# Splitting dense products into 256-column halves, full-row score products, and merged value products in a two-layer encoder kernel

## The chip, the cores and the metric

The kernel runs on one core of a Trainium2 chip. The metric is the device time of one execution in microseconds (us); lower is better. The core's engines are named as in the profile: PE does matrix products, PEld is its load of the stationary operand (which overlaps PE), DVE and ACT do element-wise work, POOL is a third element-wise engine, SP only issues DMA transfers.

## What is computed

Two layers over 512 tokens of width 1024. Each layer is an attention block and a SwiGLU feed-forward block, each with an RMS norm ahead and a residual add behind; a last norm ends it.

```python
def reference(x, norm_mix, norm_ffn, w_qkv_a, w_out_a, sink_a, w_qkv_b, w_out_b,
              w_gate, w_up, w_down, norm_final):
    for i in range(DEPTH):                      # DEPTH = 2
        h = rmsnorm(x, norm_mix[i])
        j = i // 2
        if i % 2 == 0:
            x = x + window_gqa_sink(h, w_qkv_a[j], w_out_a[j], sink_a[j])
        else:
            x = x + dilated_mixture_attention(h, w_qkv_b[j], w_out_b[j])
        h = rmsnorm(x, norm_ffn[i])
        x = x + swiglu(h, w_gate[i], w_up[i], w_down[i])
    return rmsnorm(x, norm_final)

def swiglu(h, w_gate, w_up, w_down):            # 1024 -> 2816 -> 1024
    return (jax.nn.silu(h @ w_gate) * (h @ w_up)) @ w_down
```

Layer 0's attention has 16 query heads on 4 key heads of width 64, a window of 128 keys either side, a bias linear in distance and a sink logit per head. Layer 1's has 16 heads in three groups (near keys, every 4th, every 16th), merged by their softmax denominators.

## The kernel before

All data lies transposed, features in the 128 partitions and the 512 tokens along the row. Every float32 operand of a dense product is held as two float32r tiles, a high part and the rest: `xh, xl` for the normalised input, `oh, ol` for attention outputs, `ah, al` for the feed-forward's middle, `wh, wl` for weights. Weights arrive in 128x1024 pieces by a DMA from SP into `wraw`; `split` makes `wh` on ACT (L85) and `wl` on DVE (L86), three pieces deep.

`mm3` (L106) is every dense product: high by high, high by low, low by high, three matmuls into one PSUM bank. In `unit` (projections, gate, up) and in the down and output products the weights are stationary and 512 tokens stream, so L107 to L109 are 128x512 matmuls. In `values` (L178) the tokens are stationary and 256 weight columns stream, so they are 128x256 there; `final` (L438) also runs the last down product in two column halves.

The order on PE is written out by hand; the other engines' order comes from a scheduler. Attention is a list of small steps (scores, `turn` = transposes of probabilities, `weigh` = values times probabilities), and `weave` deals them out with a fixed number of dense pieces, the fill, spread evenly between the steps: with fewer steps each gap holds more fill. The feed-forward blocks are dense products without anything between.

`score_pair` (L126) computes two heads' scores. The 64 rows of a head hold the query's high part, the other 64 its low part (`split_queries`), so that one product over 128 rows with the key's high part in both halves gives two terms. The third, query high by key low, is a product over 64 rows (L130), whose low part `kl` is one tile for both heads. `weigh`, `weigh_a` and `weigh_b` multiply 64 value columns each, in plain float32, into the upper or lower half of the one PSUM bank `ov` (L366, L658, L662, L733). In layer 0 they come one key block at a time, in layer 1 one query tile or class at a time.

In the pool `const` the tiles lie in the order in which they are declared (L72 to L81). The weights' tiles lie behind them.

Of the kernel before, what the change touches and what calls it, by code (L numbers as in the profile page):

```python
# [14 lines left out]
S = 512  # L15
# [42 lines left out]
def trunk(ctx, tc, xT, gains, sink, tabs, qsc, wunits, wv, outT):  # L58
# [11 lines left out]
        return psum.tile([128, 512], F32, tag=tag, name=name or tag, bufs=BUFS[tag])  # L70

    x = const.tile([128, NK, S], F32, name="x")  # L72
    xh = const.tile([128, NK, S], F32R, name="xh")
    xl = const.tile([128, NK, S], F32R, name="xl")
    g_sb = const.tile([128, 5, NK], F32, name="g_sb")
    qs_sb = const.tile([128, 16], F32, name="qs_sb")
    sink_sb = const.tile([128, H], F32, name="sink_sb")
    nsink = const.tile([128, H], F32, name="nsink")
    tab = const.tile([128, 1024], F32, name="tab")
# [24 lines left out]
        return chunks(tiles, shape)  # L104

    def mm3(out, ah, al, bh, bl, first, last):  # L106
        nc.tensor.matmul(out, ah, bh, start=first, stop=False)  # L107
        nc.tensor.matmul(out, ah, bl, start=False, stop=False)  # L108
        nc.tensor.matmul(out, al, bh, start=False, stop=last)  # L109

# [9 lines left out]
    def split_keys(k, pair, low):  # L120
        for a, (own, other) in enumerate((HALVES, HALVES[::-1])):
            nc.scalar.activation(pair[a][own], k[own], AF.Copy)
            nc.scalar.activation(pair[a][other], pair[a][own].bitcast(F32), AF.Copy)
            nc.vector.tensor_tensor(low[own], k[own], pair[a][own].bitcast(F32), op=OP.subtract)

    def score_pair(outs, qp, kp, low, qc, kc, first=True):  # L126
        for a in range(2):
            nc.tensor.matmul(outs[a], qp[a][:, qc], kp[a][:, kc], start=first, stop=False, skip_group_check=True)  # L128
        for a, own in enumerate(HALVES):
            nc.tensor.matmul(outs[a], qp[a][own, qc], low[own, kc], start=False, stop=True, skip_group_check=True)  # L130

# [154 lines left out]
    with tc.tile_pool(name="l0", bufs=2) as pool:  # L286
# [5 lines left out]
        def k_unit(P, **kw):  # L292
            def done(ps):
                t = spool.tile([128, S], F32, name="tmp")
                nc.vector.tensor_tensor(t, ps, norm["rb"], op=OP.mult)
                qk["k", P] = [pool.tile([128, S], F32R, name=f"kt{a}") for a in range(2)]
                qk["kl", P] = pool.tile([128, S], F32R, name="kl")
                split_keys(t, qk["k", P], qk["kl", P])
            return unit(5 * P, xh, xl, "mm", done, **kw)

# [9 lines left out]
        def attention0(P, h, b):  # L310

            k0, k1 = max(128 * b - 128, 0), min(128 * b + 256, S)
            w = k1 - k0
            off = k0 - (128 * b - 128)
            nb = w // 128
            block = slice(128 * b, 128 * b + 128)
            own = slice(4 * P + 2 * h, 4 * P + 2 * h + 2)
            heads = [8 * P + 4 * hf + 2 * h + i for i in range(2) for hf in range(2)]
            st = {}

            def scores(i):
                if i == 0:
                    st["pr"] = pool.tile([128, 4, 385], F32, name="pr", bufs=3)
                    st["m"] = pool.tile([128, 3, 4], F32, name="mst", bufs=4)
                    for k in range(2):
                        at = heads[2 * k]
                        nc.gpsimd.tensor_copy(st["pr"][:, 2 * k:2 * k + 2, w], sink_sb[:, at:at + 5:4])
                pr, m = st["pr"], st["m"]
                es = slice(2 * i, 2 * i + 2)
                ps = [bank("sc")[:, :w] for _ in range(2)]  # L330
                score_pair(ps, qk["q", P, 2 * h + i], qk["k", P], qk["kl", P], block, slice(k0, k1))
                for hf in range(2):
                    e = 2 * i + hf
# [25 lines left out]

            def weigh(kb):  # L360
                if kb == 0:
                    st["ov"] = bank("ov")
                ov = st["ov"]
                for hf in range(2):
                    vs = slice(64 * (2 * P + hf), 64 * (2 * P + hf) + 64)
                    nc.tensor.matmul(ov[64 * hf:64 * hf + 64, :256], v0[:, k0 // 128 + kb, vs],  # L366
                                     st["pt", kb][:, 256 * hf:256 * hf + 256], start=(kb == 0), stop=(kb == nb - 1))
                if kb == nb - 1:
                    src = ov[:, :256].rearrange("p (i q) -> p i q", i=2)
                    nc.scalar.activation(oh[:, own, block], src, AF.Copy)  # L370
                    nc.vector.tensor_tensor(ol[:, own, block], src, oh[:, own, block].bitcast(F32),
                                            op=OP.subtract)

            rest = [lambda kb=kb: turn(kb) for kb in range(nb)]
            rest += [lambda kb=kb: weigh(kb) for kb in range(nb - 1)]
            return [lambda: scores(0), lambda: scores(1)], rest, lambda: weigh(nb - 1)


        gens = [k_unit(0, cuts=(0, 2, 4, 8))[1], q_unit(0, 0, cuts=(0, 4, 8))[1]]
# [170 lines left out]
    with tc.tile_pool(name="l1", bufs=2) as pool:  # L550
# [9 lines left out]
        def qk_units(p, g):  # L560
# [15 lines left out]
            def k_done(ps):  # L576
                name = "k1" if g else "ka"
                qk["k", p, g] = k = pool.tile([128, S], F32, name=name, bufs=2 if g else 1)
                out, src, rb = views(k, ps, norm["rb"])
                nc.vector.tensor_tensor(out, src, rb, op=OP.mult)  # L580
                if g == 0:
                    qk["ks", p] = [pool.tile([128, S], F32R, name=f"ks{a}", bufs=1) for a in range(2)]
                    qk["kl", p] = pool.tile([128, S], F32R, name="kl1", bufs=1)
                    split_keys(k, qk["ks", p], qk["kl", p])

            at = u1 + 6 * p + 2 * g
# [182 lines left out]
        def attention_a(p):  # L769

            pts = {}

            def turn(ts, t):
                pts[t] = turn_a(p, ts, t)

            return [lambda: scores_a(p, (0, 1)), 0, lambda: scores_a(p, (2, 3)), 0,
                    lambda: turn((0, 1), 0), lambda: turn((0, 1), 1), lambda: weigh_a(p, 0, pts[0]),
                    lambda: weigh_a(p, 1, pts[1]), lambda: turn((2, 3), 2), lambda: turn((2, 3), 3),
                    lambda: merge_turn(p), lambda: weigh_a(p, 2, pts[2]), lambda: weigh_a(p, 3, pts[3]),
                    lambda: merge_back(p)]  # L780

        def attention_b(p, pauses=(0, 0, 0, 0, 0)):
            pts = {}

            def turn(cs, c):
                pts[c] = turn_b(p, cs, c)

            return [lambda: scores_b(p, (0, 1)), pauses[0], 0, lambda: scores_b(p, (2, 3)), pauses[1],
                    lambda: turn((0, 1), 0), lambda: turn((0, 1), 1), pauses[2], lambda: weigh_b(p, 0, pts[0]),
                    lambda: weigh_b(p, 1, pts[1]), pauses[3], lambda: turn((2, 3), 2), lambda: turn((2, 3), 3),  # L790
                    pauses[4], lambda: merge_rows(p), lambda: weigh_b(p, 2, pts[2]),
                    lambda: weigh_b(p, 3, pts[3])]

        def out_part(j, lo, hi, ps={}, w={}):
            def gen():
# [134 lines left out]
```

## Time and profile before

| what | value |
|---|---|
| time, median of 3 runs | 1534.75 us (1534.73 to 1535.71) |
| time of the profiled execution | 1534.25 us |
| its span, first to last instruction | 1532.5 us |
| PE busy | 1516.9 us, 8038 matmuls |
| DVE busy | 721.7 us |
| ACT busy | 606.8 us |
| granted PE clock, mean over the span | 0.997 |
| DMA | 127.68 MB, mean 83 GB/s |

Durations of PE's matmuls overlap, since they are pipelined. What a matmul costs in a stream of its kind is the distance from its start to the next one's start; the timeline's first column has the starts. "x8" at a row's end merges that many matmuls of one line. A plain float32 matmul stands in the trace as two, so a step of four of them in the program is x8 there; transposes stand as one.

### The profile page before, as it was taken

To read this page: it belongs to the slowest core of one execution; us is meant where nothing else is said; L and a number is where in the kernel's file an instruction comes from. 1 tells how busy PE (TensorE), PEld (TensorE's weight loads), DVE (VectorE), ACT (ScalarE), POOL (GpSimd) and SP (SyncE) were. 2 spreads that over 40 slices of the span, in tenths; PEclk is the share of its full clock that TensorE was granted. 3 is DMA by queue.
4 is the path that set the end of the run, shared out by engine and by line. 5 is a ranking of instruction groups with operands and counts; after the bars stand their busy time and mean duration, and the time that the engine had idled before them with its cause. 6 is when DMAs were issued, how large, how long until landed. Compare 5 with 4: busy or idle time off the path is not lost.

```text
span 1532.5 us, 19975 instructions
## 1 busy us (share of the span) xinstructions
PE 1516.9 (99%) x8038; PEld 1212.6 (79%) x8038; DVE 721.7 (47%) x1360; ACT 606.8 (40%) x1106; POOL 107.9 (7%) x151
## 2 busy tenths in 40 slices
PE   9999999999999999999999999999999999999997
PEld 7666788888888889897887877778778888888886
DVE  6666544444443343335545545545464444443223
ACT  6656443222223244443544535535443222222221
POOL 3324200000000010000000000000020000000111
PEclk9999999999999999999999999999999999999999
DMA  5110222223222232222212122222132222222231
GB/s 193 56 51 19 83 84 96 97 96 96 96 86 90 96 100 83 89 65 82 70 56 83 56 83 70 69 70 70 55 97 83 96 96 96 96 91 92 90 100 55
DMA packets 38413, 127.68 MB, mean 83 GB/s; under 512 B 4528, under 2 KB 6832, under 8 KB 38320
## 3 DMA queue, kind: packets, MB, share of 16 engines
q1 hardware_dynamic: 36832, 125.08, 24.9%
q8 instruction: 63, 1.03, 0.3%
q10 hardware_dynamic: 1488, 1.33, 0.3%
q14 instruction: 30, 0.25, 0.1%
HBM read 124.29 MB, written 2.10 MB: 82 GB/s over the span
## 4 chain that ended last, share of the span: by engine, by line
PE 97%; DVE 1%; ACT 1%; issue 0%; DMA 0%; SPq 0%; DVEq 0%; ACTq 0%
PE mm L107 18%; PE mm L109 17%; PE mm L108 17%; PE sc L109 5%; PE sc L108 5%; PE sc L107 5%; PE psv L107 4%; PE psv L109 3%; PE psv L108 3%; PE tp L107 3%; PE tp L108 3%; PE tp L109 3%; PE ov L366 1%; PE sc L128 1%; PE sc L130 1%; PE ov L733 1%
## 5 line engine op out<-in xcount | busy, mean ns | idle before, releaser
L85 ACT ACTIVATE wh<-wraw 128x1024 fp32r<-128x1024 f32 (+3 forms) x239 | 246.4, 1034 | 588.2 <-PE mm L108 228.1
L86 DVE TENSOR_TENSOR wl<-wraw,wh 128x1024 fp32r<-128x1024 f32 (+3 forms) x239 | 288.9, 1210 | 202.8 <-ACT wh L85 202.8
L107 PE MATMUL mm<-xh,wh 128*128 128x512 f32 x816 | 341.2, 418 | 0.0
L109 PE MATMUL mm<-xh,wl 128*128 128x512 f32 x816 | 323.6, 397 | 1.5 <-DVE wl L86 1.5
L108 PE MATMUL mm<-xl,wh 128*128 128x512 f32 x816 | 323.0, 396 | 0.8 <-DVE xl L206 0.8
L107 PEld LDWEIGHTS mm<-xh,wh 128*128 128x128 f32 x816 | 154.0, 189 | 49.9 <-issue 16.7
L109 PEld LDWEIGHTS mm<-xh,wl 128*128 128x128 f32 x816 | 153.8, 188 | 38.5 <-DVE wl L86 2.2
L108 PEld LDWEIGHTS mm<-xl,wh 128*128 128x128 f32 x816 | 154.4, 189 | 30.9 <-DVE xl L206 3.0
L220 POOL TENSOR_TENSOR ssum<-ssum,tmp 128x512 f32<-128x512 f32 x34 | 55.4, 1628 | 1038.9 <-ACT tmp L216 1023.9
L107 PE MATMUL psv<-wh,xh 128*128 128x256 f32 x288 | 85.3, 296 | 0.0
L109 PE MATMUL psv<-wh,xl 128*128 128x256 f32 x288 | 81.0, 281 | 0.0
L108 PE MATMUL psv<-wl,xh 128*128 128x256 f32 x288 | 80.9, 281 | 0.0
L107 PE MATMUL mm<-ah,wh 128*128 128x512 f32 (+1 forms) x198 | 75.8, 383 | 0.0
L108 PE MATMUL mm<-al,wh 128*128 128x512 f32 (+1 forms) x198 | 75.6, 382 | 0.0
L109 PE MATMUL mm<-ah,wl 128*128 128x512 f32 (+1 forms) x198 | 75.6, 382 | 0.0
L107 PE MATMUL sc<-xh,wh 128*128 128x512 f32 x176 | 69.6, 396 | 0.0
L107 PE MATMUL tp<-xh,wh 128*128 128x512 f32 x176 | 69.6, 396 | 0.0
L108 PE MATMUL tp<-xl,wh 128*128 128x512 f32 x176 | 69.5, 395 | 0.0
L109 PE MATMUL sc<-xh,wl 128*128 128x512 f32 x176 | 69.5, 395 | 0.0
L109 PE MATMUL tp<-xh,wl 128*128 128x512 f32 x176 | 69.5, 395 | 0.0
L108 PE MATMUL sc<-xl,wh 128*128 128x512 f32 x176 | 69.5, 395 | 0.0
L107 PE MATMUL sc<-ah,wh 128*128 128x512 f32 (+1 forms) x176 | 66.9, 380 | 0.0
(174 smaller groups left out, 2431.2 us busy)
## 6 DMA issues: line engine op xcount, KB each, us to landing
wraw<-wunits SPq DMA_DIRECT2D x192, 512.0 KB, 3.3
wraw<-wv SPq DMA_DIRECT2D x26, 512.0 KB, 3.3
wraw<-wunits SPq DMA_DIRECT2D x16, 384.0 KB, 2.9
x<-xT SPq DMA_DIRECT2D x8, 256.0 KB, 5.0
wraw<-wunits SPq DMA_DIRECT2D x3, 256.0 KB, 5.5
outT<-x ACTq DMA_DIRECT2D x2, 384.0 KB, 2.7
tab<-tabs SPq DMA_DIRECT2D x1, 512.0 KB, 5.9
outT<-x ACTq DMA_DIRECT2D x2, 256.0 KB, 2.3
```

The source lines that it names most:

```text
L85: nc.scalar.activation(out_h, src, AF.Copy)
L86: nc.vector.tensor_tensor(out_l, src, out_h.bitcast(F32), op=OP.subtract)
L107: nc.tensor.matmul(out, ah, bh, start=first, stop=False)
L108: nc.tensor.matmul(out, ah, bl, start=False, stop=False)
L109: nc.tensor.matmul(out, al, bh, start=False, stop=last)
L128: nc.tensor.matmul(outs[a], qp[a][:, qc], kp[a][:, kc], start=first, stop=False, skip_group_check=True)
L130: nc.tensor.matmul(outs[a], qp[a][own, qc], low[own, kc], start=False, stop=True, skip_group_check=True)
L220: nc.gpsimd.tensor_tensor(norm["sum"], norm["sum"], sq, op=OP.add)
L366: nc.tensor.matmul(ov[64 * hf:64 * hf + 64, :256], v0[:, k0 // 128 + kb, vs], st["pt", kb][:, 256 * hf:256 * hf + 256], start=(kb == 0), s ...
L733: nc.tensor.matmul(ov[rows, 128 * c:128 * c + 128], vals[p // 2, 1 + g][:, c, hv + 64 * a:hv + 64 * a + 64], pt[:, 256 * a + 128 * g:256 * ...
```

## The change

There are four edits. `mm3` issues each 512-column matmul as two of 256 columns, with the same stationary operand for both. The 64-byte tile `qs_sb` is declared ahead of `xh`, so that `xh` and `xl` lie 64 bytes further on, while all tiles from `sink_sb` on, weights and pools included, lie where they lay. `kl` becomes two tiles with the key's low part in both halves of the rows (ACT copies it across), and `score_pair` runs four products over 128 rows, which also adds the term low by low. All of a unit's or a pair's `weigh` products are issued together, and steps are reordered for it.

```diff
     x = const.tile([128, NK, S], F32, name="x")
+    qs_sb = const.tile([128, 16], F32, name="qs_sb")
     xh = const.tile([128, NK, S], F32R, name="xh")
...
     def mm3(out, ah, al, bh, bl, first, last):
-        nc.tensor.matmul(out, ah, bh, start=first, stop=False)
-        nc.tensor.matmul(out, ah, bl, start=False, stop=False)
-        nc.tensor.matmul(out, al, bh, start=False, stop=last)
+        for k, (a, b) in enumerate(((ah, bh), (ah, bl), (al, bh))):
+            for c in range(0, out.shape[-1], 256):
+                cols = slice(c, c + 256)
+                nc.tensor.matmul(out[:, cols], a, b[:, cols], start=first and k == 0 and c == 0,
+                                 stop=last and k == 2, skip_group_check=True)
...
-            nc.vector.tensor_tensor(low[own], k[own], pair[a][own].bitcast(F32), op=OP.subtract)
+            nc.vector.tensor_tensor(low[a][own], k[own], pair[a][own].bitcast(F32), op=OP.subtract)
+            nc.scalar.activation(low[a][other], low[a][own].bitcast(F32), AF.Copy)
...
         for a in range(2):
-            nc.tensor.matmul(outs[a], qp[a][:, qc], kp[a][:, kc], start=first, stop=False, skip_group_check=True)
-        for a, own in enumerate(HALVES):
-            nc.tensor.matmul(outs[a], qp[a][own, qc], low[own, kc], start=False, stop=True, skip_group_check=True)
+            for k in (kp, low):
+                nc.tensor.matmul(outs[a], qp[a][:, qc], k[a][:, kc], start=first and k is kp, stop=k is low,
+                                 skip_group_check=True)
...
             return [lambda: scores_b(p, (0, 1)), pauses[0], 0, lambda: scores_b(p, (2, 3)), pauses[1],
-                    lambda: turn((0, 1), 0), lambda: turn((0, 1), 1), pauses[2], lambda: weigh_b(p, 0, pts[0]),
-                    lambda: weigh_b(p, 1, pts[1]), pauses[3], lambda: turn((2, 3), 2), lambda: turn((2, 3), 3),
-                    pauses[4], lambda: merge_rows(p), lambda: weigh_b(p, 2, pts[2]),
-                    lambda: weigh_b(p, 3, pts[3])]
+                    lambda: turn((0, 1), 0), lambda: turn((0, 1), 1), pauses[2], lambda: turn((2, 3), 2),
+                    lambda: weigh((0, 1)), pauses[3], lambda: turn((2, 3), 3), pauses[4],
+                    lambda: merge_rows(p), lambda: weigh((2, 3))]
```

`attention_a` is reordered in the same way (its two bursts stand behind the third transposes and at the end), and layer 0's `weigh` runs over all key blocks of a unit, behind the first transposes of the next unit.

The first scores of layer 0 on PE, before (kt are the keys' high parts, kl their low part, qt the queries; two heads are one pair of tiles):

```order
L128 MATMUL sc<-kt_278,qt_289 128x256
L128 MATMUL sc<-kt_279,qt_290 128x256
L130 MATMUL sc<-kl,qt_289 128x256
L130 MATMUL sc<-kl,qt_290 128x256
L107 MATMUL mm<-xh,wh 128x512
```

The same place now, with the dense row behind it:

```order
L133 MATMUL sc<-kt_350,qt_364 128x256
L133 MATMUL sc<-kl_352,qt_364 128x256
L133 MATMUL sc<-kt_351,qt_365 128x256
L133 MATMUL sc<-kl_353,qt_365 128x256
```

The two products over 64 rows at the end of each pair are gone; each head's two products now follow each other and share the stationary queries.

The last attention pass of layer 1 on PE (p = 7), from its transposes of probabilities (L720) on, before. L733 are the value products, L765 the transposes that merge the groups:

```order
L720 MATMUL tp<-ident,pr_9067 128x128 x8
...
L733 MATMUL ov<-pt_9165,v_8095 64x128 x2
L733 MATMUL ov<-pt_9165,v_8484 64x128 x2
L733 MATMUL ov<-pt_9172,v_8095 64x128 x2
L733 MATMUL ov<-pt_9172,v_8484 64x128 x2
...
L720 MATMUL tp<-ident,pr_9105 128x128 x8
```

And now, where L722 are the transposes and L735 the value products:

```order
L722 MATMUL tp<-ident,pr_12277 128x128 x8
...
L722 MATMUL tp<-ident,pr_12321 128x128 x4
L735 MATMUL ov<-pt_12399,v_11050 64x128 x2
L735 MATMUL ov<-pt_12399,v_11532 64x128 x2
L735 MATMUL ov<-pt_12406,v_11050 64x128 x2
L735 MATMUL ov<-pt_12406,v_11532 64x128 x2
...
L722 MATMUL tp<-ident,pr_12321 128x128 x4
```

The third transposes, which need the second pair of classes (pr_12321), moved ahead of the first value products. Between them and the first transposes stands one piece of fill; before, it was one piece, the value products and three more pieces.

The split of layer 0's first key and queries on ACT, before (L122 and L123 make the keys' high parts, L117 the queries'):

```order
L122 ACTIVATE kt_278<-tmp 64x512
L122 ACTIVATE kt_279<-tmp 64x512
L123 ACTIVATE kt_278<-kt_278 64x512
L123 ACTIVATE kt_279<-kt_279 64x512
L117 ACTIVATE qt_289<-tmp 64x512
```

And now:

```order
L125 ACTIVATE kt_350<-tmp 64x512
L125 ACTIVATE kt_351<-tmp 64x512
L126 ACTIVATE kt_350<-kt_350 64x512
L128 ACTIVATE kl_352<-kl_352 64x512
L126 ACTIVATE kt_351<-kt_351 64x512
L128 ACTIVATE kl_353<-kl_353 64x512
L120 ACTIVATE qt_364<-tmp 64x512
```

Two copies of low parts come in ahead of the queries, each of which waits for DVE's subtraction.

More of the change, by code (lines that the diff above doesn't have):

```diff
@@ L75, in trunk @@
     g_sb = const.tile([128, 5, NK], F32, name="g_sb")
-    qs_sb = const.tile([128, 16], F32, name="qs_sb")
     sink_sb = const.tile([128, H], F32, name="sink_sb")
@@ L296, in done @@
                 qk["k", P] = [pool.tile([128, S], F32R, name=f"kt{a}") for a in range(2)]
-                qk["kl", P] = pool.tile([128, S], F32R, name="kl")
+                qk["kl", P] = [pool.tile([128, S], F32R, name=f"kl{a}") for a in range(2)]
                 split_keys(t, qk["k", P], qk["kl", P])
@@ L358, in turn, with weigh @@
                     nc.scalar.activation(pt, tp, AF.Copy)
[L360 to L372, printed above, removed]
+            def weigh():
+                ov = bank("ov")
+                for kb in range(nb):
+                    for hf in range(2):
+                        vs = slice(64 * (2 * P + hf), 64 * (2 * P + hf) + 64)
+                        nc.tensor.matmul(ov[64 * hf:64 * hf + 64, :256], v0[:, k0 // 128 + kb, vs],
+                                         st["pt", kb][:, 256 * hf:256 * hf + 256], start=(kb == 0),
+                                         stop=(kb == nb - 1))
+                src = ov[:, :256].rearrange("p (i q) -> p i q", i=2)
+                nc.scalar.activation(oh[:, own, block], src, AF.Copy)
+                nc.vector.tensor_tensor(ol[:, own, block], src, oh[:, own, block].bitcast(F32), op=OP.subtract)
             rest = [lambda kb=kb: turn(kb) for kb in range(nb)]
-            rest += [lambda kb=kb: weigh(kb) for kb in range(nb - 1)]
-            return [lambda: scores(0), lambda: scores(1)], rest, lambda: weigh(nb - 1)
+            return [lambda: scores(0), lambda: scores(1)], rest, weigh
         gens = [k_unit(0, cuts=(0, 2, 4, 8))[1], q_unit(0, 0, cuts=(0, 4, 8))[1]]
@@ L582, in k_done @@
                     qk["ks", p] = [pool.tile([128, S], F32R, name=f"ks{a}", bufs=1) for a in range(2)]
-                    qk["kl", p] = pool.tile([128, S], F32R, name="kl1", bufs=1)
+                    qk["kl", p] = [pool.tile([128, S], F32R, name=f"kl{a}", bufs=1) for a in range(2)]
                     split_keys(k, qk["ks", p], qk["kl", p])
@@ L774, in turn, with weigh @@
                 pts[t] = turn_a(p, ts, t)
+            def weigh(ts):
+                for t in ts:
+                    weigh_a(p, t, pts[t])
             return [lambda: scores_a(p, (0, 1)), 0, lambda: scores_a(p, (2, 3)), 0,
[L777 to L780, printed above, removed]
+                    lambda: turn((0, 1), 0), lambda: turn((0, 1), 1), lambda: merge_turn(p),
+                    lambda: turn((2, 3), 2), lambda: weigh((0, 1)), lambda: turn((2, 3), 3),
+                    lambda: merge_back(p), lambda: weigh((2, 3))]
         def attention_b(p, pauses=(0, 0, 0, 0, 0)):
@@ L786, in turn, with weigh @@
                 pts[c] = turn_b(p, cs, c)
+            def weigh(cs):
+                for c in cs:
+                    weigh_b(p, c, pts[c])
             return [lambda: scores_b(p, (0, 1)), pauses[0], 0, lambda: scores_b(p, (2, 3)), pauses[1],
-                    lambda: turn((0, 1), 0), lambda: turn((0, 1), 1), pauses[2], lambda: weigh_b(p, 0, pts[0]),
-                    lambda: weigh_b(p, 1, pts[1]), pauses[3], lambda: turn((2, 3), 2), lambda: turn((2, 3), 3),
-                    pauses[4], lambda: merge_rows(p), lambda: weigh_b(p, 2, pts[2]),
-                    lambda: weigh_b(p, 3, pts[3])]
+                    lambda: turn((0, 1), 0), lambda: turn((0, 1), 1), pauses[2], lambda: turn((2, 3), 2),
+                    lambda: weigh((0, 1)), pauses[3], lambda: turn((2, 3), 3), pauses[4],
+                    lambda: merge_rows(p), lambda: weigh((2, 3))]
         def out_part(j, lo, hi, ps={}, w={}):
```

## The prediction

> **What bounds the kernel now.** I read the page's busy times and its chain of waits first, then the groups by shape, then the timeline of PE.
>
> ```profile
> PE 1516.9 (99%) x8038; PEld 1212.6 (79%) x8038; DVE 721.7 (47%) x1360; ACT 606.8 (40%) x1106; POOL 107.9 (7%) x151
> PE 97%; DVE 1%; ACT 1%; issue 0%; DMA 0%; SPq 0%; DVEq 0%; ACTq 0%
> ```
>
> PE is busy all the time and 97% of the chain is PE. So the time is the sum of the distances between PE's starts, and an edit is worth what it does to these distances. The next rows count the dense products.
>
> ```profile
> L107 PE MATMUL mm<-xh,wh 128*128 128x512 f32 x816 | 341.2, 418 | 0.0
> L107 PE MATMUL sc<-xh,wh 128*128 128x512 f32 x176 | 69.6, 396 | 0.0
> L107 PE MATMUL tp<-xh,wh 128*128 128x512 f32 x176 | 69.6, 396 | 0.0
> L107 PE MATMUL mm<-ah,wh 128*128 128x512 f32 x176 | 69.5, 395 | 0.0
> L107 PE MATMUL sc<-ah,wh 128*128 128x512 f32 x154 | 60.8, 395 | 0.0
> L107 PE MATMUL mm<-oh,wh 128*128 128x512 f32 x128 | 53.1, 415 | 0.0
> L107 PE MATMUL psv<-wh,xh 128*128 128x256 f32 x288 | 85.3, 296 | 0.0
> ```
>
> L107 is one of three lines, so there are 3 x 1626 = 4878 matmuls of 512 columns, and 3 x 288 = 864 value matmuls of 256 columns with xh or xl. By the code 2112 of the 4878 are gate and up, 990 down, 384 output projections; the other 1392 are queries and keys, most of them woven into attention. The means here (395 ns) are latencies. What one costs is in the starts:
>
> ```profile
> 299.76 0.40 PE L108 MATMUL sc<-xl,wh 128*128 128x512 f32 x1
> ...
> 302.79 0.40 PE L109 MATMUL sc<-xh,wl 128*128 128x512 f32 x1
> ...
> 28.44 0.28 PE L109 MATMUL psv<-wh,xl 128*128 128x256 f32 x1
> ...
> 36.63 0.28 PE L109 MATMUL psv<-wh,xl 128*128 128x256 f32 x1
> ...
> 1504.39 0.28 PE L107 MATMUL sc<-ah,wh 128*128 128x256 f32 x1
> ...
> 1511.76 0.28 PE L109 MATMUL sc<-ah,wl 128*128 128x256 f32 x1
> ...
> 586.23 0.28 PE L108 MATMUL psv<-wl,oh 128*128 128x256 f32 x1
> ...
> 626.81 0.28 PE L109 MATMUL psv<-wh,ol 128*128 128x256 f32 x1
> ...
> 582.50 0.60 PE L258 MATMUL rrow<-ident,rstd 128*128 128x128 f32 x4
> ...
> 583.18 0.28 PE L109 MATMUL psv<-wh,ol 128*128 128x256 f32 x1
> ...
> 585.65 0.28 PE L109 MATMUL psv<-wh,ol 128*128 128x256 f32 x1
> ...
> 1514.28 0.58 PE L224 MATMUL ssq<-ones,tmp 128*128 128x1 f32 x4
> ...
> 1515.05 0.28 PE L109 MATMUL mm<-ah,wl 128*128 128x256 f32 x1
> ...
> 1517.17 0.28 PE L109 MATMUL mm<-ah,wl 128*128 128x256 f32 x1
> ```
>
> In pairs of first and last: 512 columns, 13 steps in 3.03 us, **233.1 ns**. 256 columns with xh, 69 steps in 8.19 us, **118.7 ns**. With ah, 65 steps in 7.37 us, **113.4 ns**; with oh, 358 steps in 40.58 us, **113.4 ns**. With oh again, 21 steps in 2.47 us, and with ah, 18 steps in 2.12 us: both **117.7 ns**. So two halves cost 226.7, 235.5 or 237.4 ns against 233.1: the gain hangs on the step that the halves fall into.
>
> In the built program xh and xl lie a whole number of 128-byte steps from the weights' tiles; ah, al, oh and ol lie 64 bytes off such a step. The 118.7 goes with the first, the 113.4 and 117.7 with the second. The shift puts xh and xl where the others are, so I expect 113.4 or 117.7 everywhere and 118.7 nowhere. Which of the two? Each of the slow stretches starts right behind plain float32 matmuls (the transposes at 582.50, the sums of squares at 1514.28) and is short; the first ended where PE waited (from 585.65 to 586.23, two steps in 0.58 us). The fast stretches started behind that wait and behind 512-column matmuls, and the long one kept its step over fourteen ends of an accumulation (24 halves each).
>
> **The change part by part.** *Dense halves.* The feed-forward and output products (3486) run long and without other work between. Each stretch starts behind float32 matmuls, so in the slow step, but ends an accumulation every 48 halves; I take it that one such end sets it right, as the wait did, and that it then stays. They gain 3486 x (233.1 - 226.7) = **22.3 us**. The 1392 woven products stand in runs of 6 to 24 halves behind float32 work, too short to recover: 1392 x (235.5 - 233.1) = 3.3 us lost. The 864 value matmuls with xh gain 864 x 1.0 = 0.9 us. The bounds are all fast, another 1392 x 8.8 + 864 x 4.3 = 16 us gained, and all slow, 3486 x 8.8 = 31 us lost.
>
> The Trainium skill, "TensorE: Matmul & The Clock Gate", section "Back-to-back issue gap", speaks against this edit: an isolated matmul takes its columns at 2.4 GHz and 2.5 ns on top. By it two halves pay that twice and lose 2.5 ns per product, 12 us in all (estimate), and the sum would be near 1523. The trace disagrees with ah and oh (226.7 under 233.1) and agrees in sign with xh (237.4).
>
> *Bursts.* A visit of `weigh` is priced from the last dense start ahead to the second one behind, less two dense steps:
>
> ```profile
> 650.29 0.40 PE L109 MATMUL mm<-xh,wl 128*128 128x512 f32 x1
> 650.62 0.66 PE L662 MATMUL ov<-pt,va 128*64 128x128 f32 x8
> ...
> 651.54 0.39 PE L108 MATMUL mm<-xl,wh 128*128 128x512 f32 x1
> ...
> 106.24 0.39 PE L109 MATMUL mm<-xh,wl 128*128 128x512 f32 x1
> 106.56 1.08 PE L366 MATMUL ov<-pt,v 128*64 128x256 f32 x8
> ...
> 107.92 0.39 PE L108 MATMUL mm<-xl,wh 128*128 128x512 f32 x1
> ```
>
> A single one costs 1.25 - 0.47 = 0.78 us, two together (the second group, two key blocks) 1.68 - 0.47 = 1.21 us: 0.35 us is paid per visit for going to half-wide products and back. Layer 0 goes from 35 visits to 16, layer 1 from 62 to 32, by the two orders. 49 x 0.35 = **17.3 us** gained.
>
> *Full-row scores.* The same reckoning:
>
> ```profile
> 634.98 0.39 PE L109 MATMUL mm<-xh,wl 128*128 128x512 f32 x1
> ...
> 635.54 0.39 PE L130 MATMUL sc<-kl,qs 64*128 64x256 f32 x2
> ...
> 636.94 0.39 PE L108 MATMUL mm<-xl,wh 128*128 128x512 f32 x1
> ...
> 45.11 0.39 PE L109 MATMUL mm<-xh,wl 128*128 128x512 f32 x1
> ...
> 46.49 0.39 PE L108 MATMUL mm<-xl,wh 128*128 128x512 f32 x1
> ```
>
> Two pairs of 256 keys cost 1.96 - 0.47 = 1.49 us, so one 0.75; one of 384 keys 1.38 - 0.47 = 0.91. No row shows four full-row products in a row; by dense steps they take 4 x 113.4 to 118.7 ns, 0.45 to 0.48 us, and with 384 columns, between 118.7 and 233.1 ns each, about 0.70. With 40 pairs and 16 pairs: 40 x 0.28 + 16 x 0.21 = 14.6 us. Some pairs shared the way back with a `weigh` beside them; I take **13 us**. At the price of the pair as it was, the gain would be nothing; that is the lower bound.
>
> *The copies of the low part* are 20 more of this form on ACT:
>
> ```profile
> L123 ACT ACTIVATE ks<-ks 64x512 fp32r<-64x512 f32 x16 | 10.1, 630 | 0.4
> ...
> 699.96 1.39 DVE L124 TENSOR_TENSOR kl<-ka,ks 64x512 fp32r<-64x512 f32 x2
> ...
> 702.51 0.50 PE L128 MATMUL sc<-ks,qs 128*128 128x256 f32 x2
> ...
> 737.73 0.84 PE L681 MATMUL sc<-k,q 64*128 64x128 f32 x12
> ...
> 746.88 1.69 ACT L712 ACTIVATE pr<-pr,mb 128x256 f32<-128x256 f32 x4
> ...
> 1108.80 1.71 ACT L712 ACTIVATE pr<-pr,mb 128x256 f32<-128x256 f32 x4 [0.35 <-DVE mb L704]
> ```
>
> 20 x 0.63 = 12.6 us lie beside PE's work, on an engine busy for 40%. But in every second pass the key is ready at 701.35 and its first scores start at 702.51; two copies (1.26 us) leave PE waiting up to half a microsecond, four times; layer 0's first scores are as tight. Queued behind is all of PE's fill. **2 us** lost.
>
> *The third transposes come earlier.* They need the row sums' scaling (L712). In odd passes that ends 10 us behind the scores (738.57 to 748.57), and two of the new copies stand on ACT in the same stretch; the new order puts 4 + 2 + 5 pieces of fill at 0.7 us and two sets of transposes at 0.44 us between, 8.6 us. PE would wait 1 to 2 us, three times. In the last pass it gets there near 1108.0, and the scaling of the first half ends at 1109.7. About **6 us** lost, between 0 and 12.
>
> *The sum*: -22.3 + 3.3 - 0.9 - 17.3 - 13 + 2 + 6 = **-42 us**. Against the profiled execution's 1534.25 us (its span is 1532.5; the median of the runs is 1534.75) this gives **1492 us**.
>
> **The rivals.** *Fast everywhere*: woven runs fall into 113.4 as well. For it, the step held over 358 halves; against it, all three entries behind float32 work were slow. 1492 - 16 = 1476.
>
> *One feed-forward block stays slow*: about 1740 products x 8.8 ns, 1492 + 15 = 1507. *Both stay slow*: 1492 + 31 = 1523. For these, no slow stretch in the trace is seen to recover but at a wait, and the long blocks have none.
>
> *The shift does nothing*, and the 118.7 belongs to something else about xh. Then 3504 products lose 4.3 ns and 1374 gain 6.4 at best: 15.1 - 8.8 = +6.3 in place of -19.9, near 1518. The Trainium skill, "SBUF — State Buffer", section "Who interferes with whom", would have it so: it gives PE separate read ports for the moving and the stationary operand and says PE never waits on anyone, so an address should not matter. The trace speaks against it: the same shape takes 118.7 or 113.4 ns by where its operand lies.
>
> *Slower than before*: every half is bound by its own load of the stationary operand, which doubles in number. PEld stands at 79% now, and 4878 loads come on top of 8038. The place is every dense product. The rest of the change saves 30 and costs 8, so it decides from 4878 x (2h - 233.1) = 22 us on, at a half of **118.8 ns**. At 118.7 nothing changes (1533). If the added loads put 1.3 ns on top of that (an estimate; no row has it), a half takes 120 and the time is 1534 - 22 + 4878 x 6.9 ns = 1546.
>
> **How the numbers follow.** Mixed as forecast 0.37, fast everywhere 0.20, one block slow 0.15, both slow 0.11, no effect of the shift 0.08, halves at 118.7 everywhere 0.04, slower 0.05. The likeliest is 1492. The range takes in the fast case with its waits at nothing (1476 less 8) and the slow one at its centre: 1468 to 1523. Less than 0.2% (3 us) can't be told from no change; so faster 0.91, same 0.04, slower 0.05.
>
> **What would show it.** Start to start of halves in the feed-forward: 113.4 there confirms, 117.7 from first to last is the slow rival, over 118.5 breaks the shift's reading. Value matmuls with xh at 118.7 as before would mean that the shift does nothing. Four score products of 256 columns in 0.5 us, and a double `weigh` at 1.2 us, settle the second and third term. PE's waits ahead of the third transposes, above 12 us in total, would make the sum wrong from the other side.

## The result and the profile after

The changed kernel takes 1494.37 us (median of 4 runs, 1494.15 to 1494.66) against 1534.74 us before in the same comparison: a ratio of 0.9738, with an interval of 0.9721 to 0.9755. The profiled execution took 1494.36 us, its span is 1492.6 us. The forecast was 1492 us.

The page's busy line, and its line on the chain of waits:

```profile
PE 1470.5 (99%) x12916; PEld 1434.8 (96%) x12916; DVE 725.0 (49%) x1360; ACT 617.1 (41%) x1126; POOL 110.2 (7%) x151
PE 92%; ACT 4%; DVE 2%; issue 1%; DMA 0%; SPq 0%; DVEq 0%; ACTq 0%
```

PE issues the 4878 extra matmuls (12916 against 8038) in 46 us less of busy time. PEld has gone from 79% to 96%; whether these loads have a part in the length of a half's step, no run separates. ACT has its 20 copies (1106 to 1126) and 10 us more work. The chain now runs over ACT and DVE for 6% of the span; the view of PE's waits says what PE itself loses there (line waited at, what it waited for: total us, times, longest):

```profile
PE tp L722 <- ACT pr L714: 5.6, 4, 1.4
...
PE sc L133 <- DVE mst L338: 0.8, 1, 0.8
...
PE sc L133 <- ACT kl L128: 0.6, 4, 0.2
```

The first row is the third transposes waiting for the row sums' scaling, the second layer 0's first scores, the last the scores waiting for the low part's second copy. Together these are 7.0 us, where the forecast had 8. The list counts only idle times of more than 0.15 us behind the matmul ahead; by the starts the same waits cost more. Here is the wait for the second copy:

```profile
680.81 0.37 PE L133 MATMUL sc<-kl,qs 128*128 128x256 f32 x1
681.02 0.28 PE L133 MATMUL sc<-ks,qs 128*128 128x256 f32 x1
681.45 0.39 PE L133 MATMUL sc<-kl,qs 128*128 128x256 f32 x1 [0.15 <-ACT kl L128]
```

These are steps of 0.21 and 0.43 us, where the same scores have 0.12 in the passes without the wait. Measured from the last dense start ahead to the second one behind, such a visit takes 1.79 us against 1.28 in the other passes, which makes 2.0 us in four passes. Counted in the same way the third transposes lose 6.2 us and layer 0's first scores 0.9: about 9 us in all.

Now the dense steps, in the timeline of PE (start, length, instruction; "x2" are the two halves of one product). First the start of layer 0's feed-forward, then the output products of layer 0, then the values made from oh in layer 1:

```profile
197.97 0.60 PE L262 MATMUL rrow<-ident,rstd 128*128 128x128 f32 x4
198.32 0.49 PE L111 MATMUL sc<-xh,wh 128*128 128x256 f32 x2
198.65 0.39 PE L111 MATMUL sc<-xl,wh 128*128 128x256 f32 x2
...
207.94 0.28 PE L111 MATMUL mm<-xh,wh 128*128 128x256 f32 x1
...
153.47 0.40 PE L111 MATMUL mm<-oh,wh 128*128 128x256 f32 x2
...
163.36 0.40 PE L111 MATMUL mm<-oh,wh 128*128 128x256 f32 x2
...
585.06 0.28 PE L111 MATMUL psv<-wh,oh 128*128 128x256 f32 x1
...
594.96 0.28 PE L111 MATMUL psv<-wh,oh 128*128 128x256 f32 x1
```

From 198.65 to 207.94 there are 82 halves, **113.3 ns** each. From 153.47 to 163.36 there are 84, **117.7 ns**; from 585.06 to 594.96 again 84, 117.9 ns. I call 113.3 the fast step and 117.8 the slow one. Counted over the whole trace, start to start: both feed-forward blocks hold 113.3 ns from the third half behind the row transposes (`rrow`) to the last (3117 steps in a row in layer 0, with the first products of layer 1 behind it, and 3021 in layer 1). The output products of layer 0 and the 48 halves of gate and up right behind them hold 117.8 ns for over 320 halves, the values from oh for some 356, and the woven stretches hold one or the other, 116.0 ns in the mean. No long stretch settles at 118.7.

A pair of scores and a weighing of two tiles, each with the dense products ahead and behind:

```profile
616.67 0.39 PE L111 MATMUL mm<-xh,wl 128*128 128x256 f32 x2
616.90 0.28 PE L133 MATMUL sc<-ks,qs 128*128 128x256 f32 x1
...
618.09 0.40 PE L111 MATMUL mm<-xl,wh 128*128 128x256 f32 x2
...
667.46 0.39 PE L111 MATMUL mm<-xh,wl 128*128 128x256 f32 x2
667.77 1.09 PE L735 MATMUL ov<-pt,v 128*64 128x128 f32 x16
...
669.14 0.40 PE L111 MATMUL mm<-xl,wh 128*128 128x256 f32 x2
```

Two pairs of 256 keys (eight products from 616.90 on) cost 1.42 us less four dense halves, 0.96 us, where they cost 1.49 before. A double weighing costs 1.68 - 0.46 = 1.22 us, where two single ones cost 1.56.

### The profile page after: what moved, and what is told of

Its sections match the earlier page's. It is cut to its first block, busy times and chain, and to the rows that moved or that the text cites. A ratio compares the mean times of both kernels' runs of the same rounds, so it can differ in the third digit from the quotient of the medians.

```text
span 1492.6 us, 29764 instructions
## 1 busy us (share of the span) xinstructions
PE 1470.5 (99%) x12916; PEld 1434.8 (96%) x12916; DVE 725.0 (49%) x1360; ACT 617.1 (41%) x1126; POOL 110.2 (7%) x151
## 4 chain that ended last, share of the span: by engine, by line
PE 92%; ACT 4%; DVE 2%; issue 1%; DMA 0%; DVEq 0%; SPq 0%; ACTq 0%
PE mm L111 50%; PE sc L111 16%; PE psv L111 9%; PE tp L111 8%; PE sc L133 2%; PE ov L370 1%; PE tp L356 1%; PE sc L683 1%; PE ov L735 1%; PE tp L645 1%; PE tp L722 1%; PE ov L664 1%; ACT pr L701 1%; ACT pr L714 1%; ACT ks L125 1%
## 5 line engine op out<-in xcount | busy, mean ns | idle before, releaser
L111 PE MATMUL mm<-xh,wh 128*128 128x256 f32 x1632 | 333.0, 285 | 0.7 <-ACT xh L209 0.7
L111 PE MATMUL mm<-xh,wl 128*128 128x256 f32 x1632 | 321.4, 279 | 1.4 <-DVE wl L86 1.4
L111 PE MATMUL mm<-xl,wh 128*128 128x256 f32 x1632 | 321.3, 278 | 0.3 <-DVE xl L210 0.3
L111 PEld LDWEIGHTS mm<-xh,wh 128*128 128x128 f32 x1632 | 248.7, 189 | 8.5 <-issue 6.7
L111 PEld LDWEIGHTS mm<-xh,wl 128*128 128x128 f32 x1632 | 247.9, 189 | 1.9 <-DVE wl L86 1.8
L111 PEld LDWEIGHTS mm<-xl,wh 128*128 128x128 f32 x1632 | 248.4, 189 | 1.0 <-DVE xl L210 0.9
L111 PE MATMUL mm<-ah,wh 128*128 128x256 f32 x374 | 74.9, 277 | 0.0
L111 PE MATMUL mm<-ah,wl 128*128 128x256 f32 x374 | 74.7, 276 | 0.0
L111 PE MATMUL mm<-al,wh 128*128 128x256 f32 x374 | 74.6, 276 | 0.0
L111 PE MATMUL tp<-xh,wh 128*128 128x256 f32 x352 | 68.8, 277 | 0.0
```

What stands on the lines that cost most here:

```text
L111: nc.tensor.matmul(out[:, cols], a, b[:, cols], start=first and k == 0 and c == 0, stop=last and k == 2, skip_group_check=True)
```

## Experiments

Twelve kernels were run, in four groups that each shared a chip with the kernel before; that kernel's median moved between 1534.9 and 1536.1 us over the groups, so ratios are given beside times.

| run | us | ratio to before (95%) |
|---|---|---|
| a: change without the shift | 1523.68 | 0.9924 (0.9909 to 0.9940) |
| b: before, shift alone | 1536.83 | 1.0012 (1.0003 to 1.0021) |
| c: before, shift and halves | 1512.63 | 0.9851 (0.9838 to 0.9864) |
| d: change with whole products | 1511.79 | 0.9848 (0.9834 to 0.9861) |
| e: weights moved in place of xh | 1513.84 | 0.9861 (0.9845 to 0.9878) |
| f: xh and weights moved | 1525.53 | 0.9935 (0.9920 to 0.9950) |
| g: xh 32 bytes off | 1527.63 | 0.9950 (0.9935 to 0.9965) |
| h: weighing ahead of third transposes | 1487.00 | 0.9686 (0.9671 to 0.9700) |
| i: before, shift and scores | 1527.31 | 0.9951 (0.9937 to 0.9965) |
| k: identity moved | 1514.90 | 0.9871 (0.9856 to 0.9886) |
| m: h, one weighing per pass | 1480.47 | 0.9647 (0.9634 to 0.9660) |
| n: identity and weights moved | 1513.43 | 0.9859 (0.9842 to 0.9875) |

### The parts: a, b, c, d, i

**a.** The one line back in its old place, the rest as changed:

```diff
-    qs_sb = const.tile([128, 16], F32, name="qs_sb")
     xh = const.tile([128, NK, S], F32R, name="xh")
     xl = const.tile([128, NK, S], F32R, name="xl")
     g_sb = const.tile([128, 5, NK], F32, name="g_sb")
+    qs_sb = const.tile([128, 16], F32, name="qs_sb")
```

> The changed kernel with qs_sb declared behind g_sb again, so that xh and xl start 64 bytes earlier, where they were before the change; all else as in the changed kernel. Theory (the place of xh and xl sets the step of their halves): gate and up, queries and keys, and the values with xh go back to 118.7 ns a half; ah and oh keep 113.3 to 117.8. 2112 products x 2 x (118.7 - 113.3) = 22.8 us, 1392 x 2 x (118.7 - 117) = 4.7 us, values 864 x about 3 = 2.6 us: 1494 + 30 = 1524 us. Rival (the address does not matter, the halves alone do it): 1494 us, halves with xh at 113.3 in the feed-forward.

The same place in its timeline, in the feed-forward:

```profile
400.09 0.40 PE L111 MATMUL tp<-xh,wh 128*128 128x256 f32 x2
...
409.83 0.40 PE L111 MATMUL mm<-xh,wl 128*128 128x256 f32 x2
```

82 halves in 9.74 us, 118.8 ns, and 1523.7 us in all: the theory's number (1524). So 29 of the 40 us that the whole change brings are lost without a shift that changes no instruction. By the Trainium skill, "SBUF — State Buffer", section "Who interferes with whom", PE has its own read ports, one each for the moving and the stationary operand, and waits on no one. The section is about engines that disturb each other and says nothing of where PE's two operands lie; that their places don't matter was the prediction's inference from it, and 118.8 against 113.3 ns decides against that. Why the place matters stays open.

**b.** The same line moved in the kernel before (its diff is a's, the other way round).

> The kernel before with the shift alone; products stay whole. Theory (the place matters only to products of 256 columns): 512 columns stay at 233.1 ns, the 864 value products with xh go from 118.7 to 113.3 or 117.8: 1 to 5 us less, 1530 to 1534 us. Rival (the place matters to every product, by a few ns each): 4878 products x 5 ns = 24 us, near 1510 us. Rival (no effect): 1534.7 us.

It came out 1.5 us slower, just beyond its interval: none of the three. Whole products don't gain from the shift (a mean of 233.3 ns over the xh products against 232.7 before), and the values with xh fell into the slow step. The values with oh, whose tiles have not moved, went from 113.3 ns to 117.8, which alone is 1.6 us. The shift is worth something to halves alone.

**c.** The kernel before with the shift and the new `mm3`:

```diff
-        nc.tensor.matmul(out, ah, bh, start=first, stop=False)
...
+        for k, (a, b) in enumerate(((ah, bh), (ah, bl), (al, bh))):
+            for c in range(0, out.shape[-1], 256):
...
```

> The kernel before with the shift and the dense halves, but the old scores and the old order of the weighings. Theory (the parts add up): feed-forward 2 x 113.3 against 233.1 ns for 3102 products, -20.2 us; output products mixed, -1 us; woven at 117 ns a half, +1.3 us; values with xh -2 us: 1534.7 - 22 = 1513 us. Rival (in the old order, with twice as many visits, the feed-forward falls into the slow step): 2 x 117.8 there, 1541 us or so. Rival (the halves bring nothing without the bursts because each return to them costs more): over 1525 us.

1512.6 us, as the theory had it. Its output products of layer 0:

```profile
166.07 0.39 PE L111 MATMUL mm<-oh,wh 128*128 128x256 f32 x2
...
175.82 0.39 PE L111 MATMUL mm<-ol,wh 128*128 128x256 f32 x2
```

86 halves in 9.75 us are 113.4 ns, and they hold it to the end. The same products, with the same padding, took 117.8 in the changed kernel: what differs is the attention work that comes ahead, with its second tile for the low part.

**d.** The changed kernel with the old `mm3` (c's diff, the other way round).

> The changed kernel with whole products of 512 columns; shift, full-row scores and bursts stay. Theory (the parts add up): scores -14, bursts -17, waits and copies +7 to +8, values -2: 1534.7 - 26 = 1509 us; the dense steps are 233.1 ns. Rival (scores and bursts gain only beside halves, because the way back to whole products costs 0.35 us each time and halves don't have it): 1520 us or more.

1511.8 us. So scores and bursts, with their copies and waits, bring 25 us (d against b), 1.6 of which are the values with oh, slow in b and fast in d.

Halves bring 22.7 us alone (c against before) and only 17.4 on top of d. Most of the 5.3 us between is found in the traces. The waits of d are shorter, as the view of PE's waits has it, since its fill of whole products is slower and its transposes come later:

```profile
PE tp L719 <- ACT pr L711: 2.5, 4, 1.2
```

This wait and the two of the scores make 3.3 us in d and 7.0 in the changed kernel, 3.7 more. And the output products of layer 0, fast in c, are slow in the changed kernel, another 1.2 us. The 360 value products with oh, which are halves by nature, say nothing here: they go from 113.3 ns to 117.8 in both comparisons (before and c, d and the changed kernel), 1.6 us each time.

**i.** The kernel before with the shift, the full-row scores and their copies:

```diff
-            nc.tensor.matmul(outs[a], qp[a][:, qc], kp[a][:, kc], start=first, stop=False, skip_group_check=True)
-        for a, own in enumerate(HALVES):
-            nc.tensor.matmul(outs[a], qp[a][own, qc], low[own, kc], start=False, stop=True, skip_group_check=True)
+            for k in (kp, low):
+                nc.tensor.matmul(outs[a], qp[a][:, qc], k[a][:, kc], start=first and k is kp, stop=k is low,
+                                 skip_group_check=True)
...
+            nc.scalar.activation(low[a][other], low[a][own].bitcast(F32), AF.Copy)
```

> The kernel before with the shift and the full-row scores with their copies of the low part; whole products and the old order of the weighings. Theory (the term as the traces price it): 40 pairs x 0.27 and 16 pairs x 0.21 us, 14 us, less what pairs beside a weighing shared before, less 1 to 2 us of waiting for the second copy: 1536.8 (shift alone) - 12 = 1525 us. Rival (the copies on ACT hold up the first scores of each pass, so half of it is given back): 1530 us or more, with over 3 us of waits of the scores for ACT. Rival (all of the difference that scores and bursts have made together is the scores'): 1512 us.

9.5 us less than b. No wait of the scores for the copies stands in the view of PE's waits here, but a new one stands at layer 0's weighing:

```profile
PE ov L367 <- DVE ol L372: 2.2, 2, 1.8
```

It was 0.4 us in the kernel before. Without it the scores bring about 11 us. Counted by starts over all 48 visits that hold such scores, b takes 85.9 us and i 73.5: 12.4 us less, near the 13 of the forecast, and i's dense steps with xh, the waits in them included, give back 1.5. The single prices agree with the forecast (0.75 to 0.48 us a pair); what falls short are pairs that share a visit. The seven visits of layer 0 that hold transposes, a pair and a weighing take 17.8 us together in b and 17.3 in i. The bursts are the rest: d against i, 15.5 us. The third transposes' 2.5 us of waits lie inside, on the side of cost; on the other side are i's own wait (1.8) and the values with oh, slow in i and fast in d (1.6). So the bursts bring about 15 us where 17.3 were forecast.

### Which distance counts: e, f, g

**e and f.** Padding behind the constants moves the weights and all behind them by 64 bytes; in e with xh back in its old place, in f with xh shifted:

```diff
     ones = const.tile([128, 1], F32, name="ones")
+    pad = const.tile([128, 16], F32, name="pad")
```

> xh and xl back where they were before the change, and 64 bytes of padding behind the constants, so that the weights' tiles and all that lies behind them (ah, al, oh, ol) start 64 bytes later. Every pair of operands is then 64 bytes apart modulo 128, as in the changed kernel, but xh, ah and oh lie on whole multiples of 128 bytes and the weights do not. Theory (the distance of the two operands counts): as the changed kernel, 1494 us, feed-forward halves at 113.3 ns. Rival (the moving operand's own place counts): xh, ah and oh all at 118.7 ns: 1523.7 + (990 + 384) products x 2 x about 5 ns = 14 us, near 1537 us.

> The changed kernel with 64 bytes of padding behind the constants: xh and xl stay 64 bytes off, the weights' tiles move 64 bytes too (so the distance to xh is a multiple of 128 again), ah, al, oh and ol move onto a multiple of 128 (64 bytes from the weights). Theory (the distance counts): as the kernel without the shift, 1523.7 us, halves with xh at 118.7 ns and with ah at 113.3 to 117.8. Rival (the moving operand's own place counts): xh fast, ah and oh at 118.7: 1494 + 14 = 1508 us.

f was 1525.5 us, as the distance of the two operands has it and the moving operand's own place has not. Its feed-forward, with xh:

```profile
400.18 0.40 PE L112 MATMUL tp<-xh,wh 128*128 128x256 f32 x2
...
409.90 0.28 PE L112 MATMUL sc<-xh,wl 128*128 128x256 f32 x1
```

82 halves, 118.5 ns. e has no stretch at 118.7, so the distance is right again; but it is at 1513.8 us, 20 above the theory. Its gate and up products, and its down products:

```profile
400.13 0.40 PE L112 MATMUL tp<-xh,wl 128*128 128x256 f32 x2
...
409.79 0.40 PE L112 MATMUL mm<-xl,wh 128*128 128x256 f32 x2
...
450.24 0.39 PE L112 MATMUL mm<-al,wh 128*128 128x256 f32 x2
...
459.99 0.28 PE L112 MATMUL sc<-ah,wl 128*128 128x256 f32 x1
```

Gate and up run at 117.8 ns (82 halves in 9.66 us), in both blocks from the first half to the last, over 2016 halves each and the 41 ends of an accumulation within them; the step goes to 113.4 (86 halves in 9.75 us) where the down products begin. 2016 products x 2 x 4.45 ns = 17.9 us in the two blocks, most of the difference. So the theory's time and the rival's both fell: a distance of 64 bytes rules out 118.7, and it leaves open which of the other two steps a stretch gets.

**g.** 96 bytes of padding ahead of xh, 32 behind the constants:

```diff
     qs_sb = const.tile([128, 16], F32, name="qs_sb")
+    pad = const.tile([128, 24], F32, name="pad")
     xh = const.tile([128, NK, S], F32R, name="xh")
...
     ones = const.tile([128, 1], F32, name="ones")
+    pad2 = const.tile([128, 8], F32, name="pad2")
```

> The changed kernel with xh and xl 32 bytes off a multiple of 128 in place of 64 (96 bytes of padding ahead of xh, 32 behind the constants; weights, ah and oh keep their places modulo 128). If any distance that is not a multiple of 128 does it: 1494 us, halves with xh at 113.3 or 117.8 ns. If only 64 does it (two operands must not meet in the same 64 bytes): halves with xh at 118.7 ns or more, 1523.7 us or more. A value between would speak for a cost that falls with the distance: near 1509 us.

1527.6 us: 32 bytes do not do what 64 do. No long stretch with xh is at 113.3. Its feed-forward, in the timeline of PE:

```profile
400.13 0.40 PE L113 MATMUL tp<-xh,wh 128*128 128x256 f32 x2
...
409.98 0.28 PE L113 MATMUL mm<-xh,wh 128*128 128x256 f32 x1
```

84 halves in 9.85 us are 117.3 ns, and 117.3 over the whole block, a step that no other kernel shows. The queries' and keys' short stretches are at 118.4 in the mean; the values with xh are at 119.8 to 120.0, slower than at whole 128 bytes. The down products, whose operands are as far apart as they were, fell from 113.3 to 117.8 in both blocks, 9 of the 33 us that g takes more than the changed kernel. The padding moved the constants between xl and the weights too, the identity among them, so the step of the long blocks is not cleanly xh's doing (see k).

### What draws the step: k, n

**k.** The identity, the transposes' second operand, moves by 64 bytes, and with it the column of ones behind it:

```diff
+    pad0 = const.tile([128, 16], F32, name="pad0")
     ident = const.tile([128, 128], F32, name="ident")
     ones = const.tile([128, 1], F32, name="ones")
+    pad1 = const.tile([128, 16], F32, name="pad1")
```

> The changed kernel with the identity, which every transpose reads, 64 bytes further on (64 bytes of padding ahead of it and 64 behind; everything else keeps its place modulo 128). No dense operand moves. Theory (the step of a stretch is drawn at its entry, by how the work just ahead of it runs): stretches behind transposes change their step, the two feed-forward blocks (entered behind the row transposes) among them or the values with oh; each feed-forward block that turns slow costs 2112 to 3102 halves x 4.5 ns = 9 to 14 us: 1494 to 1522 us, by the draw. Rival (the step belongs to the operands of the stretch itself): the same steps in the same stretches, 1494 us.

1514.9 us. The entry of the feed-forward in the timeline of PE, and a later place in it:

```profile
199.70 0.60 PE L264 MATMUL rrow<-ident,rstd 128*128 128x128 f32 x4
200.05 0.48 PE L113 MATMUL sc<-xh,wh 128*128 128x256 f32 x2
200.37 0.40 PE L113 MATMUL sc<-xl,wh 128*128 128x256 f32 x2
...
400.12 0.40 PE L113 MATMUL tp<-xh,wh 128*128 128x256 f32 x2
...
409.78 0.40 PE L113 MATMUL mm<-xh,wl 128*128 128x256 f32 x2
```

No dense operand has moved, and both gate and up blocks now run at 117.8 ns (82 halves in 9.66 us) where the changed kernel has 113.3, 18 of the 20 us. So the step isn't the dense operands' own; the work ahead has a say in it. The changed kernel shows where, at the same place in layer 1:

```profile
1125.44 0.40 PE L111 MATMUL tp<-xl,wh 128*128 128x256 f32 x2
...
1130.62 0.40 PE L111 MATMUL tp<-xh,wl 128*128 128x256 f32 x2
1130.86 0.60 PE L262 MATMUL rrow<-ident,rstd 128*128 128x128 f32 x4
1131.21 0.49 PE L111 MATMUL sc<-xh,wh 128*128 128x256 f32 x2
1131.54 0.39 PE L111 MATMUL sc<-xl,wh 128*128 128x256 f32 x2
```

Ahead of the row transposes there are 44 halves in 5.18 us, 117.7 ns; behind them the same tiles run at 113.3 to the end of the block. The step is drawn at the entry. That it is the identity that counts, and not the column of ones that moved with it and that the sums of squares ahead read, no run separates.

**n.** a with k's first padding alone, so that identity and weights move together:

```diff
     xh = const.tile([128, NK, S], F32R, name="xh")
...
+    pad0 = const.tile([128, 16], F32, name="pad0")
     ident = const.tile([128, 128], F32, name="ident")
```

> xh and xl back in their places of before, with 64 bytes of padding ahead of the identity, so that the identity, the weights' tiles and all behind them start 64 bytes later. Against the changed kernel all of these (xh, identity, weights, ah, oh, probabilities, values) have the same distances from each other modulo 128, but each lies 64 bytes from where it was. Theory (only the distances count, of the two operands for the step as such, and of the identity from the weights for the draw at the entry): the feed-forward is fast as in the changed kernel, 113.3 ns, 1494 us (1492 to 1497). Rival (the identity's own place, 96 bytes past a multiple of 128, gave the fast draw): both gate and up blocks at 117.8 ns, 1513 to 1515 us.

1513.4 us, gate and up at 117.8: the theory fell. The rival doesn't stand either, since in e the identity lies where it does in the changed kernel and the block is slow. Of the four combinations tried, one is fast, and the rule for the draw stays open. That a wait sets a stretch right fell too: in n's timeline of PE the values with oh run fast behind a short wait at 575.70 (a step of 0.39 us),

```profile
584.96 0.28 PE L112 MATMUL psv<-wh,oh 128*128 128x256 f32 x1
...
594.93 0.28 PE L112 MATMUL psv<-wl,oh 128*128 128x256 f32 x1
```

88 halves at 113.3 ns, and in the changed kernel behind the same wait (at 565.19, a step of 0.40 us) at 117.9 (above).

### Faster versions: h, m

**h.** The weighing ahead of the third transposes again, in `attention_b`:

```diff
-                    lambda: turn((0, 1), 0), lambda: turn((0, 1), 1), pauses[2], lambda: turn((2, 3), 2),
-                    lambda: weigh((0, 1)), pauses[3], lambda: turn((2, 3), 3), pauses[4],
+                    lambda: turn((0, 1), 0), lambda: turn((0, 1), 1), pauses[2], lambda: weigh((0, 1)),
+                    lambda: turn((2, 3), 2), pauses[3], lambda: turn((2, 3), 3), pauses[4],
```

> The changed kernel with the weighing of the first two tiles put ahead of the third transposes in attention_b (the number of visits stays). Theory (the third transposes wait because they were moved ahead of 1.2 us of weighing and some fill): the 5.6 us of waits for the row sums' scaling fall to 0.5 or less, 1494.4 - 5 = 1489 us. Rival (the wait goes elsewhere, since the scores' work on DVE and ACT is late anyway: to the weighing of the second pair or to the merge): 1493 to 1494.5 us, with as much waiting on other lines.

1487.0 us, 7.4 less than the changed kernel. The 5.6 us at the transposes are gone from the list of waits, and the scores' wait for the copies is down to

```profile
PE sc L133 <- ACT kl L128: 0.2, 1, 0.2
```

with 0.7 us new at the weighing. That makes 5.3 by the list. By the starts the visits with these transposes are 6.5 us shorter, and the two profiled executions are 6.3 us apart (1494.36 and 1488.03); the rest is within what two comparisons on different chips can differ by. The copies still cost 2.0 us here: the scores' visits still take 1.76 us against 1.27 in the other passes, with most of the idle times too short for the list.

**m.** h, with the four tiles of a pass weighed together at its end:

```diff
-                    lambda: turn((0, 1), 0), lambda: turn((0, 1), 1), lambda: merge_turn(p),
-                    lambda: turn((2, 3), 2), lambda: weigh((0, 1)), lambda: turn((2, 3), 3),
-                    lambda: merge_back(p), lambda: weigh((2, 3))]
+                    lambda: turn((0, 1), 0), lambda: turn((0, 1), 1), lambda: merge_turn(p), 0,
+                    lambda: turn((2, 3), 2), lambda: turn((2, 3), 3),
+                    lambda: merge_back(p), lambda: weigh((0, 1, 2, 3))]
...
-                    lambda: turn((0, 1), 0), lambda: turn((0, 1), 1), pauses[2], lambda: weigh((0, 1)),
+                    lambda: turn((0, 1), 0), lambda: turn((0, 1), 1), pauses[2], 0, 0,
...
-                    lambda: merge_rows(p), lambda: weigh((2, 3))]
+                    lambda: merge_rows(p), lambda: weigh((0, 1, 2, 3))]
...
-        spread(attention_b(7, [2, 6, 1, 3, 1]), fill)
+        spread(attention_b(7, [2, 6, 4, 1, 1]), fill)
```

> The version with the weighing ahead of the third transposes, and in it all four tiles of a pass in layer 1 weighed in one visit in place of two (16 visits fewer), with fill in place of the first weighing ahead of the third transposes; in the last pass the pauses are 2, 6, 4, 1, 1. Theory (a visit costs 0.35 us for going there and back, whatever it holds): 1487.0 - 16 x 0.35 = 1481.5 us, and a visit of 32 products costs 1.22 + 0.87 = 2.1 us. Rival (the visit's length itself costs, or the later weighing holds up the merge and the next pass's scores): 1486 us or more, with new waits of 3 us or more.

One such visit in the timeline of PE:

```profile
676.61 0.39 PE L111 MATMUL mm<-xh,wl 128*128 128x256 f32 x2
676.93 1.97 PE L735 MATMUL ov<-pt,v 128*64 128x128 f32 x32
...
679.17 0.40 PE L111 MATMUL mm<-xl,wh 128*128 128x256 f32 x2
```

2.56 less 0.46 us is the 2.10 foreseen, against 2 x 1.22 for two visits, and the time is 1480.5 us, the fastest of all: 16 visits fewer, 6.5 us less, without a new wait over 1 us. The price rests on this row and not on the total, in which other things meet. The scores no longer come upon an unfinished second copy:

```profile
681.16 0.28 PE L133 MATMUL sc<-ks,qs 128*128 128x256 f32 x1
681.28 0.28 PE L133 MATMUL sc<-kl,qs 128*128 128x256 f32 x1
```

By the starts that is 1.9 us less; the weighings are 5.5 us shorter, h's new wait at the weighing is gone (0.9), and slower dense steps give back 1.3.

## Why the prediction came out

- **The shift.** Right. In the changed kernel halves with xh never settle at 118.7, and without the shift they always do (a: 29 us). The rival in which it does nothing fell; f and e show that the distance of the two operands counts, not the place of one.
- **Dense halves.** The net of -19.9 us lies between the two measured, -22.7 alone and -17.4 on top of the rest. The feed-forward was in the fast step as forecast. **The reason given for that was wrong**: "one such end sets it right". The feed-forward was fast from its third half, before any accumulation had ended; the output products of layer 0 stayed at 117.8 over six such ends, and e's gate and up over 41. Nor does a stretch behind float32 work always start slow. The step is drawn at the entry and kept until other work or a wait comes between, in e, k and n also until the operands change. So the rivals with slow blocks were real: e, k and n came between the two, with gate and up slow in both blocks and the down products fast, 1513 to 1515 us, on nothing but 64 bytes of padding. The forecast's main term rested on a draw that it had no reason to call: here it was lucky.
- **Woven halves.** Forecast slow throughout, measured mixed: the queries' and keys' are at 115.6 ns in the mean, so they gain some 2 us where 3.3 were to be lost. The output products of layer 0 (1.5 us) were forecast too bright. A term is missing from the sum: the values with oh were fast before, became slow, and lost 1.6 us.
- **Bursts.** Price and number right: 1.22 us against 1.21 foreseen for a double visit, and m's visit of 2.10 us repeats the 0.35. What they bring together, about 15 us by d and i, is 2 less than forecast.
- **Scores.** The price of a pair was right; of the 13 us, i shows 12.4 by the starts of its score visits and about 11 in its time without its own wait, and pairs that share a visit gain least.
- **Copies and transposes.** 1.4 and 5.6 us by the list of waits, 2.9 and 6.2 by the starts, against 2 and 6. h takes the transposes' wait away, which shows that they came from the order and not from the scaling being late as such.
- **Slower than before.** Fell: with PEld at 96%, no long stretch of the changed kernel ran above 119 ns a half. By the Trainium skill, "TensorE: Matmul & The Clock Gate", section "Back-to-back issue gap", two halves would lose 2.5 ns to one whole product (an estimate from its isolated gap); c differs, with 2 x 113.3 against 233.3 ns, and a agrees in sign alone, with 2 x 118.7.
- **The sum.** 1492 us against 1494.4 is closer than its terms: bursts, copies and the values with oh came out some 5 us worse than put, the woven halves some 5 better.

## What to carry to other kernels

Where PE is busy all the time, price an edit by the distances between its starts, visit by visit, and gather narrow products into few visits: the price of a visit held to some hundredths of a microsecond. Before and after any split of dense products, look at the step of each long stretch by itself: here the same products took 113.3, 117.8 or 118.7 ns by where tiles lay and by what ran ahead, up to 2% of the kernel, and an edit that moves a tile can win or lose more than what it was made for. Where a reorder brings a step ahead, count what its input still needs: moving one weighing back gave 7 us.

## What the runs showed of the hardware

- A product of 256 columns in this type has two steady steps at a distance of 64 bytes between its operands, 113.3 and 117.8 ns, and 118.7 ns at a distance of whole 128 bytes (a, f); at 32 bytes both gate and up blocks were at 117.3 and the values at 120.0 (g). Whole products of 512 columns with xh take 233.3 ns at 64 bytes (b, d) and 232.7 in the mean at whole 128 (before).
- The step of a stretch, kept over as many as 3117 halves, depends on the work ahead: moving the identity that the transposes ahead read, and the ones behind it, took both gate and up blocks from 113.3 to 117.8 ns, and the time from 1494.4 to 1514.9 us (k). What decides it is open.
- A visit of half-wide products costs 0.35 us beyond its products, whether it holds 8, 16 or 32 of them (0.78, 1.22, 2.10 us).
